# Where in memory the normalised activations of a trunk layer start: 64 and 320 bytes behind a multiple of 512 in place of 0

## The chip, the cores and the metric

The kernel runs on one core of a Trainium2 chip. The metric is the device time in microseconds (us) of one execution; the median of three timed executions of the kernel before is 1382.2 us (1381.91 to 1386.94).

## The reference

One layer of a decoder trunk for 256 positions and 2048 channels, in float32. What matters here is that two normalised activations, `h`, each feed one large projection:

```
mod = (silu(c) @ w_ada + b_ada)                    # six vectors of 2048: shift, scale, gate, twice
h = rms_norm(x, norm1_g) * (1 + scale1) + shift1
proj = h @ w_in + b_in                             # 2048 -> 8192: a_val, a_gate, u, v, g_A, g_B
y_a = silu(layer_norm(dwconv31(a_val * sigmoid(a_gate)))) @ w_conv_out
y_b = (u * spatial_mix(layer_norm(v))) @ w_sgu_out # u, v after GELU
merged = sigmoid(g_A) * y_a + sigmoid(g_B) * y_b
x = x + gate1 * (merged @ w_out)
h = rms_norm(x, norm2_g) * (1 + scale2) + shift2
up = dwconv3(h @ w_up)                             # 2048 -> 11264
x = x + gate2 * ((silu(gt) * val) @ w_down)        # 5632 -> 2048
return rms_norm(x, final_g)
```

## The kernel before

**Split operands.** A float32 product is made from TensorE products of float32r parts: every operand is split into a high part (ScalarE, L145) and a low part (VectorE, L146), and a product is three matmuls: high by high, high by low, low by high (`mm3`, L166 to L170; `mm3a`, L172 to L176). Weights come in tiles of 128 x 2048 (1 MB) by DMAs that SyncE issues (`load_raw`, L148; four buffers), and `load_split` (L155) makes their parts (tags `hi` and `lo`, three buffers each).

**h as the streamed operand.** The activations lie channel by channel: `hH` and `hL` hold 16 tiles of 128 channels x 256 positions, 1024 bytes for each tile in each partition. In the first projection a slice of 128 weight columns (512 bytes in a partition) is loaded into the array, and 256 columns of `hH` or `hL` are streamed past it: "pa" (L168 to L170, convolution branch), "pvc" and "pv" (v), "pu" (u), "pg" (gates). In the up-projection (`mm_up`, L669) the two parts of the second `h` lie side by side for each k (`h2[k]` is 2 x 256 columns): a high weight slice streams all 512 columns (L672), a low one the 256 of the high part (L673). In the output and the down projection (`proj_T`, L563) it is the other way round: slices of the activations (`mH`, `mL`, or the feed-forward's `f`) are loaded into the array, and 512 columns of the weights are streamed.

**Places.** `place(shape, dt, tag, name)` (L80) takes one tile from a pool with one buffer for each tag; tiles of one tag follow each other in the same bytes. `PADS` puts 384 bytes ahead of the first of them, tag T0, which thereby starts at byte 1536 = 3 x 512 of a partition. All the large tiles have sizes in multiples of 512 bytes, so all start at a multiple of 512: `hH` at 42,496 = 83 x 512, `hL` 16,384 bytes behind it, the weight buffers `raw`, `hi` and `lo` from 117,248 = 229 x 512 on. Tag `hH` holds in turn `hH`, `mH` (merged activations), the first half of the second `h`, and `kept0`, a weight tile of the last stage that is used twice; tag `hL` holds `hL`, `mL`, the second half, and `kept1`.

**Order of the work.** (Times are those of the profile's span.) From 20 to 200 us a loop over the 16 channel tiles makes `h` tile by tile from modulation weights (tag `ada`, multiplied on VectorE, L190) and uses each at once; in its second half each step also does two half tiles of gates. Then v, a, u and the other half of the gates (200 to 426 us), the two branch projections (to 535 us), the output projection "wo" (to 634 us), 24 blocks of the up-projection (to 902 us), a first down-projection (to 1035 us), the other 20 blocks (to 1261 us) and the last down-projection. `pump` puts background work (the taps of the convolution, L316, and the modulation columns, L190) between the blocks, each of them with a cost, so that VectorE's queue carries it in program order beside the splits of the weights.

Of the kernel before, what the change touches and what calls it, by code (L numbers as in the profile page):

```python
# [11 lines left out]
F32R = mybir.dt.float32r  # L12
# [5 lines left out]
P = 128  # L18
D = 2048
S = 256  # L20
NT = S // P
KT = D // P
# [18 lines left out]
HI_BUFS = 3  # L41

PADS = dict(T0=384)


C_C = 0
# [19 lines left out]
def trunk(ctx, tc, xin, cvec, rows, wada, wa0, wa1, wv, wu, wg, wso, wco, wsT, wout, wup0, wup, wdn, out):  # L66
# [8 lines left out]
    def psum(name="ps"):  # L75
        return pp.tile([P, 512], F32, tag="ps", name=name)

    pads = dict(PADS)

    def place(shape, dt, tag, name):  # L80

        if pads.get(tag):
            pad = big.tile([P, pads.pop(tag) // 4], F32, tag=f"pad{tag}", name=f"pad{tag}")
            nc.gpsimd.memset(pad, 0.0)
        return big.tile(shape, dt, tag=tag, name=name)

    def slot(i, shape, name, dt=F32):

        return place(shape, dt, f"T{i}", name)
# [4 lines left out]
    def t2(name):  # L94
        return tp.tile([P, 512], F32, tag="t2", name=name, bufs=4)
# [48 lines left out]
    def split(hi, lo, src):  # L144
        nc.scalar.activation(hi, src, AF.Copy)  # L145
        return nc.vector.tensor_tensor(lo, src, hi.bitcast(F32), op=ALU.subtract)  # L146
# [8 lines left out]
    def load_split(src, name, places=None):  # L155

        raw = load_raw(src, name)
        if places is None:
            hi = wp.tile([P, 2048], F32R, tag="hi", name=f"hi_{name}", bufs=HI_BUFS)
            lo = wp.tile([P, 2048], F32R, tag="lo", name=f"lo_{name}", bufs=HI_BUFS)  # L160
        else:
            hi, lo = places[:, 0, :], places[:, 1, :]
        last["split"] = split(hi, lo, raw)
        return [(hi[:, h * 1024:(h + 1) * 1024], lo[:, h * 1024:(h + 1) * 1024]) for h in range(2)]
# [7 lines left out]
    def mm3a(ps, aH, aL, wH, wL, start, stop, **kw):  # L172

        nc.tensor.matmul(ps, aH, wH, start=start, stop=False, **kw)  # L174
        nc.tensor.matmul(ps, aH, wL, start=False, stop=False, **kw)  # L175
        nc.tensor.matmul(ps, aL, wH, start=False, stop=stop, **kw)  # L176
# [3 lines left out]
    nc.scalar.activation(cact, cv[:, C_C:C_C + KT], AF.Sigmoid)  # L180
    nc.vector.tensor_tensor(cact, cact, cv[:, C_C:C_C + KT], op=ALU.mult)
    cbc = place([P, D], F32, "cbc", "cbc")
    for q in range(4):
        bcast_cols(cbc[:, q * 512:(q + 1) * 512], cact[:, 4 * q:4 * q + 4], 4, f"c{q}")
# [39 lines left out]
    def make_h(hH, hL, src, gs, sh, rrow, name):  # L224
# [2 lines left out]
        nc.scalar.activation(hH, h, AF.Identity, bias=sh)  # L227
        return nc.vector.scalar_tensor_tensor(hL, h, sh, hH.bitcast(F32), op0=ALU.add, op1=ALU.subtract)  # L228

    hH = place([P, KT, S], F32R, "hH", "hH")  # L230
    hL = place([P, KT, S], F32R, "hL", "hL")

# [18 lines left out]
    for k in range(KT):  # L253
        c = slice(k, k + 1)
# [25 lines left out]
    def pump(phase, pe, dve):  # L280

        fill, share = SHARES[phase]
        us = fill * pe - dve
        if not (bg["conv"] and bg["ada"]):
            share = 1.0 if bg["conv"] else 0.0
        for key, part in (("conv", us * share), ("ada", us * (1 - share))):
            credit[key] += part
            while bg[key] and credit[key] >= bg[key][0][0]:
                cost, f = bg[key].pop(0)
                credit[key] -= cost  # L290
                f()
            if not bg[key]:
                credit[key] = 0.0
# [243 lines left out]
    for j in range(8):  # L537
        nc.scalar.activation(ycf[:, j, :], ycf[:, j, :], AF.Silu, scale=cv[:, C_LG + j:C_LG + j + 1], bias=cv[:, C_LB + j:C_LB + j + 1])
        if j % 4 == 3:
            hs = slice(j - 3, j + 1)  # L540
            split(aH[:, hs, :], aL[:, hs, :], ycf[:, hs, :])
    mH = place([P, KT, S], F32R, "hH", "mH")
    mL = place([P, KT, S], F32R, "hL", "mL")
    for j2 in range(8):
        parts = load_split(wco[j2], f"co{j2}")
        ps = psum(f"pco{j2}")
# [16 lines left out]
    def proj_T(blk, groups, aHf, aLf, gate, after, rate, pref, apart=False):  # L563

        groups = list(groups)

        def block(ps, g, parts, ts, first, last):
            for kk in range(4):
                k = 4 * g + kk
                hi, lo = parts[kk // 2]  # L570
                cs = slice((kk % 2) * 512, (kk % 2 + 1) * 512)
                for t in ts:
                    tk = slice(t * P, (t + 1) * P)
                    mm3a(ps[t], aHf(k)[:, tk], aLf(k)[:, tk], hi[:, cs], lo[:, cs], first and kk == 0, last and kk == 3)

        def residual(ps, c, t):
            cs = slice(c * 512, (c + 1) * 512)
            tm = t2(f"res{pref}{c}{t}")
            with tc.high_priority(offset=HURRY):
                nc.vector.tensor_tensor(tm, ps[t], gate()[:, cs], op=ALU.mult)  # L580
                nc.vector.tensor_tensor(x2[t][:, cs], x2[t][:, cs], tm, op=ALU.add)
                after(c, t, cs)

        for c in range(4):
            ps = [psum(f"po{pref}{c}{t}") for t in range(NT)]
            if apart and c == 3:

                kept = {}
                for gi, g in enumerate(groups):
                    places = place([P, 2, 2048], F32R, ("hH", "hL")[gi], f"kept{gi}") if gi < 2 else None  # L590
                    kept[g] = load_split(blk(c, g), f"{pref}{c}_{g}", places)
                    block(ps, g, kept[g], [0], gi == 0, gi == len(groups) - 1)
                residual(ps, c, 0)
                order = groups[:-3:-1] + groups[:2] + groups[2:-2]
                for gi, g in enumerate(order):
                    parts = kept[g] if gi < 4 else load_split(blk(c, g), f"{pref}{c}_{g}again")
                    block(ps, g, parts, [1], gi == 0, gi == len(order) - 1)
                residual(ps, c, 1)
                break
            for gi, g in enumerate(groups):  # L600
                parts = load_split(blk(c, g), f"{pref}{c}_{g}")
                at_end = gi == len(groups) - 1
                for ts in ([0], [1]) if at_end else ([0, 1],):
                    block(ps, g, parts, ts, gi == 0, at_end)
                if rate:
                    pump("wo", 5.15, rate)
                if gi == 0:
                    while later:
                        later.pop(0)()
            with ExitStack() as behind:  # L610
                if c == 3 and pref == "wo":
                    up0.append(load_split(wup0[0], "up00"))
                    behind.enter_context(tc.issue_after(last["split"].ins))
                for t in range(NT):
                    residual(ps, c, t)
# [16 lines left out]
    while len(bg["ada"]) > 2 * KT:  # L632
        bg["ada"].pop(0)[1]()
    proj_T(lambda c, g: wout[c, g], range(4), lambda k: mH[:, k, :], lambda k: mL[:, k, :], get_gate1, after_out, 2.9, "wo")
    drain("ada")

# [8 lines left out]
    while later:  # L645
        later.pop(0)()

    h2 = [place([P, 8, 2, S], F32R, tag, f"h2{tag}") for tag in ("hH", "hL")]

    def h2_of(k):  # L650
        return h2[k // 8][:, k % 8, :, :]
# [80 lines left out]
    def down(groups, after, pref, apart=False):  # L732
        proj_T(lambda c, g: wdn[c, g], groups, lambda k: fH[k], lambda k: fL[k], get_gate2, after, 0, pref, apart)
# [89 lines left out]
```

## Time and profile before

| | before |
|---|---|
| median of the timed runs | 1382.2 us (1381.91 to 1386.94, three runs) |
| the profiled execution's own time | 1381.48 us |
| its span, first to last instruction | 1379.7 us |
| TensorE busy / VectorE busy / ScalarE busy | 1334.1 / 1072.6 / 648.8 us |
| mean granted TensorE clock | 0.987 |
| read from and written to HBM | 347.51 MB, 2.10 MB |

The profiled execution's own time is 1.8 us above its span and 0.7 us below the median. A matmul's busy time in the profile is longer than its share of the stream, since matmuls are pipelined: what a matmul costs is the distance from its start to the next one's start. PE is TensorE's matmuls, PEld its weight loads, DVE VectorE, ACT ScalarE, SP SyncE. A window's row gives the busy time of each engine in it with the number of its instructions, then the granted clock (1.00 is full speed), the mean busy share of the DMA engines, and GB/s.

### The profile page before, as it was taken

Reading aid. Unit: us, or ns where it says so; the run is one execution under the profiler, and the core shown is the slowest. Engines: PE = TensorE matmul, PEld = TensorE weight load, DVE = VectorE, ACT = ScalarE, POOL = GpSimd, SP = SyncE. Lnnn points to the kernel's source line nnn. Section 1 sums busy time; section 2 is a strip of 40 time slices with the busy share of each in tenths; the row PEclk is TensorE's granted clock in tenths of the full one; section 3 lists DMA queues with packets and bytes.
Section 4 is the critical chain, followed back from the end, with each engine's and each line's share of the span. In section 5 each row is a group of like instructions: output and inputs, shape, how many; then the busy total and the mean of one; then the engine's idle time right before and its main releaser. Section 6 shows DMA issues by size and latency. Waiting matters only on the chain.

```text
span 1379.7 us, 19691 instructions
## 1 busy us (share of the span) xinstructions
PE 1334.1 (97%) x8170; PEld 1201.4 (87%) x8170; DVE 1072.6 (78%) x1319; ACT 648.8 (47%) x772; POOL 7.0 (1%) x18
## 2 busy tenths in 40 slices
PE   5789999999999999998999999999999999999997
PEld 4689999999999899887888888888888888888885
DVE  6987789999999699788998887754556766776573
ACT  5244464544551244445555555543335555555351
POOL 0000000000000000000000000000000000000000
PEclk9899999999999999999999999999999999999998
DMA  9999977677776799895887774555555555555551
GB/s 351 382 366 326 335 306 272 229 290 270 293 284 246 278 347 345 329 341 216 308 302 279 289 287 183 185 181 197 199 184 187 189 190 190 189 184 183 189 207 61
DMA packets 49481, 350.89 MB, mean 254 GB/s; under 512 B 5488, under 2 KB 5488, under 8 KB 8432
## 3 DMA queue, kind: packets, MB, share of 16 engines
q1 hardware_dynamic: 49392, 349.63, 68.0%
q8 instruction: 64, 1.05, 0.3%
q14 instruction: 25, 0.20, 0.0%
HBM read 347.51 MB, written 2.10 MB: 253 GB/s over the span
## 4 chain that ended last, share of the span: by engine, by line
PE 93%; DVE 4%; DMA 2%; ACT 1%; issue 0%; POOL 0%; ACTq 0%; POOLq 0%; SPq 0%
PE pup L672 24%; PE pup L673 12%; PE pod L176 6%; PE pod L175 6%; PE pod L174 6%; PE pg L170 4%; PE pg L169 4%; PE pg L168 4%; PE pso L529 4%; PE powo L175 2%; PE powo L176 2%; PE powo L174 2%; DVE ada L190 2%; PE pa L168 2%; PE pa L169 2%; PE pa L170 2%
## 5 line engine op out<-in xcount | busy, mean ns | idle before, releaser
L146 DVE TENSOR_TENSOR lo_up<-raw_up,hi_up 128x2048 fp32r<-128x2048 f32 x88 | 201.6, 2290 | 84.1 <-ACT hi_up L145 84.1
L672 PE MATMUL pup<-h2hH,hi_up 128*128 128x512 f32 x704 | 252.2, 397 | 1.4 <-DVE h2hH L228 1.4
L672 PE MATMUL pup<-h2hL,hi_up 128*128 128x512 f32 x704 | 250.0, 394 | 0.0
L190 DVE SCALAR_TENSOR_TENSOR ada<-ada,cbc 128x2048 f32<-128x2048 f32 x96 | 218.7, 2286 | 15.7 <-DMA ada<-in 7.9
L145 ACT ACTIVATE hi_up<-raw_up 128x2048 fp32r<-128x2048 f32 x88 | 168.8, 1918 | 109.4 <-PE pup L672 83.1
L673 PE MATMUL pup<-h2hH,lo_up 128*128 128x256 f32 x704 | 198.3, 282 | 0.0
L673 PE MATMUL pup<-h2hL,lo_up 128*128 128x256 f32 x704 | 197.4, 280 | 0.0
L146 DVE TENSOR_TENSOR lo_d<-raw_d,hi_d 128x2048 fp32r<-128x2048 f32 x42 | 96.3, 2292 | 92.1 <-ACT hi_d L145 92.1
L672 PEld LDWEIGHTS pup<-h2hH,hi_up 128*128 128x128 f32 x704 | 133.0, 189 | 32.9 <-DVE h2hH L228 1.8
L672 PEld LDWEIGHTS pup<-h2hL,hi_up 128*128 128x128 f32 x704 | 131.9, 187 | 30.8
L170 PE MATMUL pg<-hH,lo_g 128*128 128x256 f32 x512 | 145.0, 283 | 0.4 <-DVE lo_g L146 0.4
L169 PE MATMUL pg<-hL,hi_g 128*128 128x256 f32 x512 | 144.9, 283 | 0.0
L168 PE MATMUL pg<-hH,hi_g 128*128 128x256 f32 x512 | 144.9, 283 | 0.0
L673 PEld LDWEIGHTS pup<-h2hH,lo_up 128*128 128x128 f32 x704 | 134.1, 190 | 0.0
L673 PEld LDWEIGHTS pup<-h2hL,lo_up 128*128 128x128 f32 x704 | 133.0, 189 | 0.0
L145 ACT ACTIVATE hi_d<-raw_d 128x2048 fp32r<-128x2048 f32 x42 | 80.5, 1917 | 107.1 <-PE pod L176 106.1
L175 PE MATMUL pod<-lo_d,f 128*128 128x512 f32 x332 | 129.3, 389 | 0.0
L174 PE MATMUL pod<-hi_d,f 128*128 128x512 f32 x332 | 129.2, 389 | 0.0
L176 PE MATMUL pod<-hi_d,f 128*128 128x512 f32 x332 | 129.2, 389 | 0.0
L170 PEld LDWEIGHTS pg<-hH,lo_g 128*128 128x128 f32 x512 | 98.3, 192 | 0.6 <-DVE lo_g L146 0.6
L168 PEld LDWEIGHTS pg<-hH,hi_g 128*128 128x128 f32 x512 | 98.3, 192 | 0.0
L169 PEld LDWEIGHTS pg<-hL,hi_g 128*128 128x128 f32 x512 | 98.3, 192 | 0.0
(202 smaller groups left out, 2585.4 us busy)
## 6 DMA issues: line engine op xcount, KB each, us to landing
ada<-in SPq DMA_DIRECT2D x96, 1024.0 KB, 5.5
raw_up<-in SPq DMA_DIRECT2D x88, 1024.0 KB, 4.8
raw_d<-in SPq DMA_DIRECT2D x44, 1024.0 KB, 4.8
raw_g<-in SPq DMA_DIRECT2D x32, 1024.0 KB, 5.7
raw_wo<-in SPq DMA_DIRECT2D x16, 1024.0 KB, 4.9
raw_a<-in SPq DMA_DIRECT2D x16, 640.0 KB, 5.6
raw_a<-in SPq DMA_DIRECT2D x8, 1024.0 KB, 4.8
raw_u<-in SPq DMA_DIRECT2D x8, 1024.0 KB, 4.9
```

The lines of the kernel that those rows point to most:

```text
L145: nc.scalar.activation(hi, src, AF.Copy)
L146: return nc.vector.tensor_tensor(lo, src, hi.bitcast(F32), op=ALU.subtract)
L168: nc.tensor.matmul(ps, wH, aH, start=start, stop=False, **kw)
L169: nc.tensor.matmul(ps, wH, aL, start=False, stop=False, **kw)
L170: nc.tensor.matmul(ps, wL, aH, start=False, stop=stop, **kw)
L174: nc.tensor.matmul(ps, aH, wH, start=start, stop=False, **kw)
L175: nc.tensor.matmul(ps, aH, wL, start=False, stop=False, **kw)
L176: nc.tensor.matmul(ps, aL, wH, start=False, stop=stop, **kw)
L190: nc.vector.scalar_tensor_tensor(w, w, 1.0, cbc, op0=ALU.mult, op1=ALU.mult, accum_out=dst)
L529: nc.tensor.matmul(ps[:, half * S:(half + 1) * S], raw[:, c0:c0 + P], uv[:, k, :], start=(k == 0), stop=(k == 7))
L672: nc.tensor.matmul(ps, hi, hk.rearrange("p a s -> p (a s)"), start=(k == 0), stop=(k == KT - 1), skip_group_check=True)
L673: nc.tensor.matmul(ps[:, :S], lo, hk[:, 0, :], start=False, stop=(k == KT - 1), skip_group_check=True)
```

## The change

The two tags become one, `hh`, of 8192 + 128 float32 columns (33,280 bytes, 65 x 512), and a helper cuts two areas of 16,384 bytes out of it that start at a chosen byte. The first `h` starts 64 bytes behind a multiple of 512, the second 320 bytes, the merged activations and the kept weights at 0. All four users name it:

```
+H_AT, H2_AT = 64, 320
...
+    def pair(names, by, inner=(S,)):
+
+        t = place([P, 8192 + 128], F32R, "hh", "_".join(names))
+        two = [t[:, by // 4 + i * 4096:by // 4 + (i + 1) * 4096] for i in range(2)]
...
-    hH = place([P, KT, S], F32R, "hH", "hH")
-    hL = place([P, KT, S], F32R, "hL", "hL")
+    hH, hL = pair(("hH", "hL"), H_AT)
...
-    mH = place([P, KT, S], F32R, "hH", "mH")
-    mL = place([P, KT, S], F32R, "hL", "mL")
+    mH, mL = pair(("mH", "mL"), 0)
...
+                room = pair(("kept0", "kept1"), 0, (2048,))
...
-    h2 = [place([P, 8, 2, S], F32R, tag, f"h2{tag}") for tag in ("hH", "hL")]
+    h2 = pair(("h2a", "h2b"), H2_AT, (2, S))
```

The tile itself stays at 42,496. What lies behind it moves by 512 bytes, so every other large tile still starts at a multiple of 512, and the small ones keep their distance from one. Each engine issues the same instructions in the same order, with waits on the same engines and DMA queues: nothing but addresses differs between the two programs.

More of the change, by code (lines that the diff above doesn't have):

```diff
@@ L85, in place @@
         return big.tile(shape, dt, tag=tag, name=name)
+    def pair(names, by, inner=(S,)):
+        t = place([P, 8192 + 128], F32R, "hh", "_".join(names))
+        two = [t[:, by // 4 + i * 4096:by // 4 + (i + 1) * 4096] for i in range(2)]
+        if len(inner) == 1:
+            return [x.rearrange("p (a b) -> p a b", b=inner[0]) for x in two]
+        return [x.rearrange("p (a b c) -> p a b c", b=inner[0], c=inner[1]) for x in two]
     def slot(i, shape, name, dt=F32):
@@ L588, in proj_T @@
                 kept = {}
+                room = pair(("kept0", "kept1"), 0, (2048,))
                 for gi, g in enumerate(groups):
-                    places = place([P, 2, 2048], F32R, ("hH", "hL")[gi], f"kept{gi}") if gi < 2 else None
+                    places = room[gi] if gi < 2 else None
                     kept[g] = load_split(blk(c, g), f"{pref}{c}_{g}", places)
```

## The prediction

> **What bounds the kernel now.** The page comes first: the share of TensorE in the span and in the chain of work that ended last.
>
> ```profile
> PE 1334.1 (97%) x8170; PEld 1201.4 (87%) x8170; DVE 1072.6 (78%) x1319; ACT 648.8 (47%) x772; POOL 7.0 (1%) x18
> PE 93%; DVE 4%; DMA 2%; ACT 1%; issue 0%; POOL 0%; ACTq 0%; POOLq 0%; SPq 0%
> L672 PE MATMUL pup<-h2hH,hi_up 128*128 128x512 f32 x704 | 252.2, 397 | 1.4 <-DVE h2hH L228 1.4
> L170 PE MATMUL pg<-hH,lo_g 128*128 128x256 f32 x512 | 145.0, 283 | 0.4 <-DVE lo_g L146 0.4
> ```
>
> TensorE carries 93% of the chain, and its large groups waited 1.4 and 0.4 us in all. So the pace of the matmul stream is the time, wherever another engine could follow a faster one. Whether it could is read by stage, from the windows.
>
> ```profile
> 20.00:113.00 93.00, 74.18 (x518) 70.50 (x519) 83.98 (x98) 31.11 (x30) 0.00 (x0) 0.90 0.97 364
> 113.00:200.00 87.00, 87.00 (x727) 87.00 (x726) 68.76 (x71) 43.71 (x48) 1.56 (x1) 1.00 0.87 324
> 208.00:236.00 28.00, 28.00 (x237) 28.00 (x236) 28.00 (x40) 11.77 (x14) 0.00 (x0) 1.00 0.72 270
> 290.00:330.00 40.00, 40.00 (x336) 40.00 (x335) 39.99 (x58) 19.49 (x21) 0.00 (x0) 1.00 0.77 274
> 340.00:400.00 60.00, 60.00 (x502) 60.00 (x502) 59.64 (x76) 33.26 (x39) 0.00 (x0) 1.00 0.80 297
> 660.00:860.00 200.00, 200.00 (x1155) 176.36 (x1154) 172.18 (x222) 111.94 (x152) 0.00 (x0) 1.00 0.74 275
> 1045.00:1245.00 200.00, 200.00 (x1134) 173.44 (x1133) 139.65 (x177) 109.60 (x141) 0.00 (x0) 1.00 0.52 187
> ```
>
> The columns after the length are PE, PEld, DVE, ACT and POOL. Up to 113 us TensorE has gaps and the DMA engines are 97% busy. From 113 us on TensorE has none. From 200 to 426 us (third to fifth row) VectorE has none either: 28.00 of 28, 39.99 of 40, 59.64 of 60. In the up-projection (last two rows) VectorE has 14% and 30% to spare, and the DMA engines more.
>
> What one matmul costs is the distance between starts. Two starts in the gate stage, with the six between them left out, and two early in the loop, with six left out, where the clock stood at half:
>
> ```profile
> 344.74 0.28 PE L168 MATMUL pg<-hH,hi_g 128*128 128x256 f32 x1
> ...
> 345.58 0.28 PE L169 MATMUL pg<-hL,hi_g 128*128 128x256 f32 x1
> ```
> ```profile
> 59.64 0.41 PE L168 MATMUL pa<-hH,hi_a 128*128 128x256 f32 x1
> ...
> 61.13 0.41 PE L170 MATMUL pa<-hH,lo_a 128*128 128x256 f32 x1
> ```
> ```profile
> 59.60:61.20 1.60, 1.60 (x10) 1.60 (x9) 1.53 (x5) 0.40 (x1) 0.00 (x0) 0.50 0.88 317
> ```
>
> At half clock 256 columns take 1.49 / 7 = 0.2129 us, so at full clock the stream itself would need some 106.4 ns (an estimate: half of it). The gate stage takes 0.84 / 7 = 120.0 ns: **13.6 ns for each matmul are no streaming**, and they are absent at half clock. The up-projection shows the same for its pairs of 512 and 256 columns:
>
> ```profile
> 660.00:860.00 200.00, 200.00 (x578) 107.89 (x577) 1.00 0.74 275
> 1045.00:1245.00 200.00, 200.00 (x567) 106.35 (x567) 1.00 0.52 187
> ```
>
> These are the windows for L672 alone, one such matmul in each pair. A pair takes 200 / 577 = 346.6 ns in the first 24 blocks and 200 / 567 = 352.7 ns in the other 20, where 768 columns need 319.3 by the same estimate: 27.3 and 33.4 ns are lost. Instructions, operands' starts modulo 512 and clock are the same in the two windows, and the other engines do less in the second. So the loss depends on how the weight load and the stream beside it fall against each other in time. Behind a short interruption at 200.6 us it also changes for a while:
>
> ```profile
> 200.97 0.28 PE L169 MATMUL pvc<-hL,hi_v 128*128 128x256 f32 x1
> ...
> 201.80 0.28 PE L170 MATMUL pvc<-hH,lo_v 128*128 128x256 f32 x1
> ```
>
> Seven distances of 0.83 / 7 = 118.6 ns, before the stage settles at 120 again.
>
> **The change part by part.** Only addresses differ, so nothing is removed, added or queued otherwise; each step is a price per instruction.
>
> Writing `h` at another start costs nothing on VectorE and ScalarE, as far as the nearest rows tell: the convolution's taps read `apad` at starts that step by 4 bytes, and their durations hardly spread.
>
> ```profile
> L316 DVE SCALAR_TENSOR_TENSOR yc<-apad,cv,yc x200: 430/479/486, 192.2 to 444.1; 128x256 f32<-128x256 f32 x100
> L228 DVE SCALAR_TENSOR_TENSOR hL<-h,sh,hH x16: 476/479/481, 20.6 to 181.7; 128x256 fp32r<-128x256 f32 x16
> ```
>
> The taps' median of 479 ns is that of the aligned writes of `hL`. If all 32 writes of `h` lost 10 ns it would be 0.3 us. The shift by 512 of all that lies behind, the merged activations and the kept weights keep their places modulo 512: nothing.
>
> What is left is the streamed read of `h` beside the loading of weights. Now both start at a multiple of 512 each time. A weight slice is 512 bytes; the stream of 256 columns is 1024 bytes. If the two disturb each other where they pass the same place modulo some 512 bytes, they now meet at the start, and the stream, which passes more bytes in the same time, laps the slice once before its end. With a start 64 or 320 bytes on, the first meeting is gone and the lapping is left. That is argued, not seen: no row shows a float32r stream that starts elsewhere. The bounds per matmul: the loss goes (13.6 ns gained), or it grows, by the nearest row as the second up window did against the first (6.1 ns a pair). I take half of it gone, 6.8 ns for each matmul that streams `h`.
>
> The Trainium skill (SBUF — State Buffer, "SBUF: two separate sides" and "Who interferes with whom") says that TensorE reads the streamed operand and the weights through two independent ports, that loading the next weights takes nothing from the running matmul, and that TensorE never waits on anyone. By that rule the start of `h` could not matter, and the sum below would be 0; it is the second rival. The trace speaks against its full form, since the pair's price above moves by 6.1 ns with no change of instruction or start.
>
> The Trainium skill (TensorE: Matmul & The Clock Gate, "Back-to-back issue gap") gives N / 2.4 + 2.5 ns at full clock, 109.2 ns for 256 columns. The gate stage's 120.0 ns do not agree; with that floor instead of 106.4 a full removal would be worth 10.8 and not 13.6 ns.
>
> The sum, stage by stage:
>
> - 20 to 113 us: the DMA engines set the pace, 0.
> - 113 to 200 us: 727 matmuls x 6.8 ns = 4.9 us. The DMA engines must then bring 324 x 87 / 82.1 = 343 GB/s, and the first window shows 364. So 4.9.
> - 200 to 426 us: pvc, pa, pu and pg have 288 + 384 + 384 + 768 = 1824 such matmuls, 12.4 us on TensorE; but VectorE has no gap, and TensorE can only draw nearer to it. How near it is:
>
> ```profile
> L170 PE MATMUL pg<-hH,lo_g x512: 283/283/385, 83.4 to 426.3; 128*128 128x256 f32 x171
> L146 DVE TENSOR_TENSOR lo_g<-raw_g,hi_g x32: 2283/2291/2294, 81.1 to 411.6; 128x2048 fp32r<-128x2048 f32 x32
> L146 DVE TENSOR_TENSOR aL<-yc,aH x2: 1218/1222/1226, 480.9 to 486.4; 128x1024 fp32r<-128x1024 f32 x2
> L168 PE MATMUL pco<-aH,hi_co x128: 278/283/468, 488.7 to 534.5; 128*128 128x256 f32 x128
> ```
>
> The last low part is ready at 411.6 + 2.3 = 413.9 us; its 48 matmuls x 120 ns start at about 426.4 - 5.8 = 420.6. The cushion is 6.7 us, and no more can be gained. At the branch projection the operand `aL` is done at 487.6, 1.1 us ahead of its first use, so some is given back there. I count 4.
> - 634 to 902 us: 24 blocks x 2 x 16 = 768 pairs x 13.65 ns = 10.5 us. VectorE's 172 us in 200 fit into 192.
> - 1035 to 1261 us: 640 pairs from 352.7 to the same 333.0 ns, 19.7 each, 12.6 us.
> - wo, the two down-projections and the branch projections stream other operands: 0.
>
> Together 32.0 us off the profiled execution's 1381.5 leaves 1349.5. It lies 0.7 below the median of the runs shown, so **1350 us**. Behind the up-projection the down stages have TensorE alone on the chain, so what is gained there stays.
>
> **The rivals.**
>
> *All of the loss goes.* For: at half clock there is none. Against: then the lapping would cost nothing either. 727 x 13.6 = 9.9, which the DMA engines' 364 GB/s hold to 9; 5 for 200 to 426 us; 768 x 27.3 = 21.0; 640 x 33.4 = 21.4: 56 us, 1326.
>
> *It doesn't do what it says: the 13.6 ns are a price of each matmul that no start moves.* For: 512-column pairs and 256-column matmuls lose the same per matmul, 27.3 / 2 and 13.6. Against: the second up window and the 118.6 ns. 1382.
>
> *Slower: the stream locks into a worse rhythm.* The second up window shows one, at the same starts. If a start 320 bytes on leads the first 24 blocks into it, 768 x 6.1 = 4.7 us; if the other 20 lose as much again, 640 x 6.1 = 3.9; and 3 ns on each of the 727 + 1824 matmuls that stream the first `h`, which nothing hides since TensorE has no gap there, 7.7. Together 16 us, 1398. It decides from about 5 ns a pair on: 1408 x 5 = 7 us.
>
> **How the numbers follow.** A measurement of this kernel can tell about 0.5% (6.9 us) from no change. Half of the loss gone: 0.50. All gone: 0.13. No effect: 0.20. Slower: 0.17. So faster 0.63, same 0.20, slower 0.17. The forecast's own range is 1335 to 1370 (about three quarters of the loss gone to a quarter). The range of 8 in 10 reaches from 1327, about the case of all gone, up to 1388, over no effect and its 0.5%; it leaves out most of the slower case and a part of the fastest.
>
> **What would show it right or wrong.** Right: in the gate stage the distance between starts falls from 120 to some 113 ns, or at least comes to stand on VectorE's splits, with waits of "pg" for `lo_g`; in both up windows L672 counts about 600 in 200 us; wo and down keep theirs. The half is wrong if the count is 577 and 567 again (no effect), above 620 (all gone) or below 560 (slower). The cap of 200 to 426 us is wrong if that stretch shortens by more than 7 us.

## The result, and the profile after

The changed kernel takes 1376.58 us (median of six, 1374.36 to 1379.05) where the kernel before takes 1384.57 (median of six, 1381.47 to 1389.23): ratio 0.9941, 95% interval 0.9916 to 0.9965. It is faster, as forecast, but by 8 us, a quarter of the 32 that the sum gave: 6.6 us above the upper end of the forecast's own range (1335 to 1370), inside the range of 8 in 10 (1327 to 1388). The profiled execution took 1376.01 us, its span 1374.3.

Start of the page of the changed kernel (its lines stand 9 further on, so L168 to L170 are now L177 to L179, L672 is L680), and the windows that answer to those of before:

```profile
PE 1327.7 (97%) x8170; PEld 1195.6 (87%) x8170; DVE 1073.5 (78%) x1319; ACT 649.8 (47%) x772; POOL 6.9 (1%) x18
PE 93%; DVE 3%; DMA 3%; ACT 1%; issue 0%; POOL 0%; ACTq 0%; POOLq 0%; SPq 0%
```
```profile
20.00:113.00 93.00, 73.05 (x510) 69.55 (x511) 83.72 (x97) 30.49 (x30) 0.00 (x0) 0.89 0.96 359
113.00:200.00 87.00, 87.00 (x741) 87.00 (x740) 70.10 (x71) 44.46 (x49) 1.56 (x1) 1.00 0.88 330
340.00:400.00 60.00, 60.00 (x512) 60.00 (x511) 60.00 (x74) 32.61 (x41) 0.00 (x0) 1.00 0.79 297
```

From 113 us on the same stretches hold more matmuls: 741 for 727, 512 for 502. A window also counts the matmuls that began ahead of it and are still running, 0.28 / 0.12 or some 2.4 of them, so the gate stage goes from 60 / 499.6 = 120.1 ns a matmul to 60 / 509.6 = 117.7. The forecast had 113.2. The up-projection, L680 alone:

```profile
660.00:860.00 200.00, 200.00 (x574) 107.89 (x574) 1.00 0.73 269
1045.00:1245.00 200.00, 200.00 (x575) 107.89 (x574) 1.00 0.53 187
```

578 and 567 counted pairs have become 574 and 575. From start to start a pair takes 348.9 ns in both parts; before it took 346.7 in the first and 353.3 in the second (the prediction's 352.7 took 567 pairs for that window, one too many). So the first part has become slower and the second quicker. The distances between the starts of L680 (L672 before) repeat themselves: 347, 347, 346 ns in the first part of before, 361, 349, 350 in its second, 351, 349, 347 after. Such a repeating pattern is called a rhythm below. From the first starts of the groups in both traces:

| stretch | before, us | after, us | difference |
|---|---|---|---|
| up to the first "pvc" | 200.8 | 200.1 | -0.7 |
| v, a, u, gates | 225.7 | 221.1 | -4.6 |
| so, co, wo | 207.4 | 207.7 | +0.3 |
| up-projection, 24 blocks | 268.5 | 270.9 | +2.4 |
| first down-projection | 132.4 | 132.3 | -0.1 |
| up-projection, 20 blocks | 226.1 | 223.3 | -2.8 |
| rest | 118.8 | 118.9 | +0.1 |
| span | 1379.7 | 1374.3 | -5.4 |

Of the +2.4 us in the first part, 768 x 2.2 ns = 1.7 are the pairs' price. The other 0.7 lie in the first block, whose first pairs run at half clock (640 ns each): it took 445 ns a pair after and 422 before. The first row of the table is uncertain by more than its 0.7 us: over the profiles of all experiments it is 200.8 to 202.4 us with the first `h` at 0 and 198.1 to 200.1 with it at 64.

VectorE did not become the limit. Its cushion in the gate stage:

```profile
L179 PE MATMUL pg<-hH_hL,lo_g x512: 279/280/384, 84.9 to 421.1; 128*128 128x256 f32 x171
L155 DVE TENSOR_TENSOR lo_g<-raw_g,hi_g x32: 2287/2302/2924, 82.6 to 410.1; 128x2048 fp32r<-128x2048 f32 x32
```

The last low part is ready at 412.4, its 48 matmuls begin at 421.1 - 48 x 0.1177 = 415.5: 3.1 us of the 6.7 are left, and "pg" waited 0.4 us in all for `lo_g`, as before.

### The profile page after: what moved, and what is told of

Same layout as the page of the kernel before. It is cut to its first block, busy times and chain, and to the rows that moved or that the text cites. A ratio compares the mean times of both kernels' runs of the same rounds, so it can differ in the third digit from the quotient of the medians.

```text
span 1374.3 us, 19691 instructions
## 1 busy us (share of the span) xinstructions
PE 1327.7 (97%) x8170; PEld 1195.6 (87%) x8170; DVE 1073.5 (78%) x1319; ACT 649.8 (47%) x772; POOL 6.9 (1%) x18
## 4 chain that ended last, share of the span: by engine, by line
PE 93%; DVE 3%; DMA 3%; ACT 1%; issue 0%; POOL 0%; ACTq 0%; POOLq 0%; SPq 0%
PE pup L680 24%; PE pup L681 12%; PE pod L184 6%; PE pod L183 6%; PE pod L185 6%; PE pg L179 4%; PE pg L177 4%; PE pg L178 4%; PE pso L537 4%; PE powo L184 2%; PE powo L185 2%; PE powo L183 2%; DVE ada L199 2%; PE pa L179 2%; PE pa L177 2%; PE pa L178 2%
## 5 line engine op out<-in xcount | busy, mean ns | idle before, releaser
L680 PE MATMUL pup<-h2a_h2b,hi_up 128*128 128x512 f32 x1408 | 494.1, 395 | 0.9 <-DVE h2a_h2b L237 0.9
L681 PE MATMUL pup<-h2a_h2b,lo_up 128*128 128x256 f32 x1408 | 395.7, 281 | 0.0
L680 PEld LDWEIGHTS pup<-h2a_h2b,hi_up 128*128 128x128 f32 x1408 | 266.3, 189 | 62.7 <-DVE h2a_h2b L237 1.3
L681 PEld LDWEIGHTS pup<-h2a_h2b,lo_up 128*128 128x128 f32 x1408 | 265.0, 188 | 0.0
L179 PE MATMUL pg<-hH_hL,lo_g 128*128 128x256 f32 x512 | 143.2, 280 | 0.4 <-DVE lo_g L155 0.4
L177 PE MATMUL pg<-hH_hL,hi_g 128*128 128x256 f32 x512 | 143.1, 279 | 0.0
L178 PE MATMUL pg<-hH_hL,hi_g 128*128 128x256 f32 x512 | 142.8, 279 | 0.0
L179 PEld LDWEIGHTS pg<-hH_hL,lo_g 128*128 128x128 f32 x512 | 96.2, 188 | 0.6 <-DVE lo_g L155 0.6
L178 PEld LDWEIGHTS pg<-hH_hL,hi_g 128*128 128x128 f32 x512 | 96.0, 187 | 0.0
L177 PEld LDWEIGHTS pg<-hH_hL,hi_g 128*128 128x128 f32 x512 | 95.9, 187 | 0.0
L177 PE MATMUL pa<-hH_hL,hi_a 128*128 128x256 f32 x256 | 72.1, 300 | 19.6 <-ACT hH_hL L236 19.6
L155 DVE TENSOR_TENSOR lo_g<-raw_g,hi_g 128x2048 fp32r<-128x2048 f32 x32 | 74.5, 2328 | 18.5 <-ACT hi_g L154 18.5
L324 DVE SCALAR_TENSOR_TENSOR yc<-apad,cv,yc 128x256 f32<-128x256 f32 x200 | 85.7, 495 | 0.2
```

Of the source, the lines that this page charges most:

```text
L177: nc.tensor.matmul(ps, wH, aH, start=start, stop=False, **kw)
L178: nc.tensor.matmul(ps, wH, aL, start=False, stop=False, **kw)
L179: nc.tensor.matmul(ps, wL, aH, start=False, stop=stop, **kw)
L324: nc.vector.scalar_tensor_tensor(ycf[:, j, :], src, cv[:, w0 + k:w0 + k + 1], ycf[:, j, :], op0=ALU.mult, op1=ALU.add)
L680: nc.tensor.matmul(ps, hi, hk.rearrange("p a s -> p (a s)"), start=(k == 0), stop=(k == KT - 1), skip_group_check=True)
L681: nc.tensor.matmul(ps[:, :S], lo, hk[:, 0, :], start=False, stop=(k == KT - 1), skip_group_check=True)
```

## The experiments

Theory A: a float32r stream and the loading of the next weights disturb each other by their distance in memory and by their distance in time; the start changes a small part of the loss, and the up-projection's pairs have several rhythms. The rivals are named in the expectations. Eight kernels are timed against before, in three batches of five rounds, each beside executions of before of its own; four are streams without the layer, profiled once. So every price of a pair or a matmul is that of one profiled execution.

### One step alone

The edits are the one line, in turn (both at 0; only the first moved; only the second moved):

```
-H_AT, H2_AT = 64, 320
+H_AT, H2_AT = 0, 0       # zero
+H_AT, H2_AT = 64, 0      # h64
+H_AT, H2_AT = 0, 320     # h2only
```

> One place, but both h at 0: only the merging of the two tags and the shift of all that lies behind by 512 bytes are left. Theory A (the start of the streamed operand against the weights' changes a small part of what each matmul loses): as before, 120.0 ns a matmul in the gate stage, pairs of the up-projection at 346.6 or 352.7 ns, a time within 0.3% of before. Rival B (the one place or the shift by 512 did it): 117.7 ns and 348.5 ns as in the changed kernel, some 8 us faster.

Measured: ratio 0.9993 (0.9976 to 1.0010), the gate stage at 120 ns and pairs at 346.7 and 353.3. Rival B falls: the one place and the shift by 512 do nothing that can be measured.

> Only the first h moved, to 64; the second at 0. Theory A: 117.7 ns in the gate stage, and pairs in one of the rhythms of before, 346.6 or 352.7 ns; some 5 us faster than before where the rhythms are the same. Rival B: the same as with both at 0.

Measured: ratio 0.9952 (0.9931 to 0.9973), median 1375.92. The gate stage of zero and then of h64:

```profile
340.00:400.00 60.00, 60.00 (x502) 60.00 (x502) 59.81 (x77) 31.70 (x38) 0.00 (x0) 1.00 0.80 297
```
```profile
340.00:400.00 60.00, 60.00 (x512) 60.00 (x511) 59.82 (x74) 32.77 (x39) 0.00 (x0) 1.00 0.77 285
```

502 matmuls as before, and 512 as in the changed kernel: 117.7 ns. The stretch of v, a, u and gates took 225.7 and 221.1 us.

> Only the second h moved, to 320; the first at 0. Theory A: 120.0 ns in the gate stage, 348.5 ns for every pair in both parts of the up-projection: 1.5 us lost in the first 24 blocks and 2.7 gained in the other 20 against the profile of before, so about 1 us faster, and up to 6 us faster than an execution of before in which both parts run at 352.7. Rival B: as with both at 0.

Measured: ratio 0.9988 (0.9972 to 1.0004), median 1384.01. The first part was not at 348.5 but at 353.3 ns, the second at 348.9. The windows of L680 (L672's heir), of h64 and then of h2only:

```profile
660.00:860.00 200.00, 200.00 (x578) 107.87 (x578) 1.00 0.73 269
1055.00:1245.00 190.00, 190.00 (x539) 101.05 (x538) 1.00 0.53 189
```
```profile
660.00:860.00 200.00, 200.00 (x567) 106.36 (x566) 1.00 0.74 273
1055.00:1245.00 190.00, 190.00 (x545) 102.42 (x545) 1.00 0.53 189
```

567 pairs in the first part of h2only, where the changed kernel, with the same second start, has 574. As far as the times can tell, the whole of the gain comes from the first `h`; the second start of 320 has no effect that can be told from none, and two prices of its own.

### Streams without the layer

Matmuls alone, all operands ready beforehand; a case is a pair of starts, and each is interrupted by 128-column transposes. The core of the first of them:

```
for name, form, h, w in PLAN:
    for part in range(2):
        upset(name)                       # a 128-column transpose
        for b in range(8):
            ...
            for k in range(4):            # hi, lo: weights at WA[w]; hk: h at HA[h]
                ...
                nc.tensor.matmul(ps[:, :S], hi, hk[:, 0, :], ...)
                nc.tensor.matmul(ps[:, :S], hi, hk[:, 1, :], ...)
                nc.tensor.matmul(ps[:, :S], lo, hk[:, 0, :], ...)
```

> A stream of its own that computes nothing of the layer: 256-column float32r matmuls in threes as in the gate stage, with no other engine at work, 192 for each case, interrupted twice by one 128-column transpose; h at 0, 32, 64, 128, 192, 256, 320, 384, 448 with the weights at 0; then weights at 64 with h at 0, 64, 128, and weights at 448 with h at 0. Theory A (the two reads disturb each other by their distance modulo 512): 120.0 ns at 0, 117.7 at 64; h and weights both at 64 give 120.0, h at 128 with weights at 64 117.7. Rival C (the start counts by itself): h and weights both at 64 give 117.7, h at 0 with weights at 64 120.0. Rival D (what is lost comes from the other engines' and the DMAs' traffic): 109 ns or less in all cases.

The starts of the two transposes of a case, 96 matmuls apart, in the trace: h at 64 with weights at 0, then both at 64, then h at 0 with weights at 64.

```profile
56.91 0.27 PE L120 MATMUL zca<-ident,xs 128*128 128x128 f32 x1
...
68.33 0.27 PE L120 MATMUL zca<-ident,xs 128*128 128x128 f32 x1
```
```profile
239.97 0.27 PE L120 MATMUL zcc<-ident,xs 128*128 128x128 f32 x1
...
251.59 0.27 PE L120 MATMUL zcc<-ident,xs 128*128 128x128 f32 x1
```
```profile
217.54 0.27 PE L120 MATMUL zac<-ident,xs 128*128 128x128 f32 x1
...
228.55 0.27 PE L120 MATMUL zac<-ident,xs 128*128 128x128 f32 x1
```

11.42, 11.62 and 11.01 us: with both at 64 the stream is as slow as with both at 0 (308.89 to 320.51, 11.62 too), 0.20 / 96 = 2.1 ns a matmul slower than with h alone at 64. So the distance counts, not the start (rival C falls), and other engines' traffic is not needed (rival D falls). Mean distances between starts behind the first 24 of a part:

| h minus weights, bytes | 256 columns, ns |
|---|---|
| 0, 256 | 120.0 |
| 64, 192, 320, 448 | 117.8 |
| 128, 384 | 118.6 |
| 32 | 116.7 |
| -64 (weights moved) | 113.3 in one part, 117.8 in the other |

> As the first stream with 256 columns in threes, finer: h at 0, 16, 32, 48, 64, 80, 96, 224, 480 with weights at 0, then h at 0 with weights at 32, 64 and 128; three interruptions for each. Theory A: 120 ns at 0, between 116 and 119.5 elsewhere, h at 224 like h at 480 (they differ by 256), weights moved up by 64 like h moved to 192 or 448. If the loss could all go at some start, one of these cases would be near 107 to 109 ns; theory A with a fixed part expects none under 113.

Measured: 16 and 32: 116.7; 48, 224, 480 and weights at 32: 118.3 to 118.4; 80 and 96: 120.0; weights at 128: 118.7; h at 64, and weights at 64: 117.8 or 113.3, by the interruption. Nothing is under 113.3. The starts 48 (116 to 119.5 expected, 118.4 found) and 224 (like 480) came out by theory A; 80 and 96, with the full 120.0, and the 113.3 did not.

> A stream that computes nothing of the layer, no other engine at work: pairs of a 512- and a 256-column float32r matmul as in the up-projection, 72 pairs for each case after each of three interruptions (one, two, three 128-column transposes), h at 0, 32, 64, 128, 192, 256, 320, 384, 448 and weights at 0; then 512-column matmuls alone, as in the down-projection, h at 0, 64, 128, 256, 320; then pairs at 0 once more. Theory A (distance modulo 256 between stream and weights sets the loss, and the pairs have several rhythms that an interruption can switch): pairs of 346.6 or 353 ns at 0 and at 256, 349 or 353 ns at 320 and at 64, and 192 and 448 like 64; 512 columns alone 226.7 ns at 0 and 256 and some 2 ns less at 64 and 320. Rival E (each start has one price, and the two prices in the kernel come from what the other engines do): one value for each case, whatever the interruption.

Measured, over whole pairs: 346.7 or 353.3 ns at 0 and at 256, by the interruption; 346.7 at 32 after all three; 353.3 at 64, 192, 320 and 448; 351.1 at 128 and 384. 512 columns alone: 226.7 at 0 and 256, 228.9 at 64 and 320, some 232 at 128, so dearer, not cheaper as expected. Pairs at 0 behind two and behind three transposes, 15 and 16 pairs apart, and at 32, 16 pairs:

```profile
425.31 0.40 PE L137 MATMUL spz<-ha,wa 128*128 128x512 f32 x1
...
430.61 0.40 PE L137 MATMUL spz<-ha,wa 128*128 128x512 f32 x1
```
```profile
433.75 0.39 PE L137 MATMUL spz<-ha,wa 128*128 128x512 f32 x1
...
439.30 0.39 PE L137 MATMUL spz<-ha,wa 128*128 128x512 f32 x1
```
```profile
41.20 0.39 PE L137 MATMUL spb<-hb,wa 128*128 128x512 f32 x1
...
46.75 0.39 PE L137 MATMUL spb<-hb,wa 128*128 128x512 f32 x1
```

5.30 / 15 = 353.3, 5.55 / 16 = 346.9, 5.55 / 16 = 346.9. Same program lines, same addresses, no other engine at work, two prices: rival E falls. The number of transposes does not choose between them: behind three, 0 gave 353.3 in the first case and 346.7 in the last. At 320, the second start of the change, the pair is at the dearer price after all three.

> Where the part of the loss comes from that no start moves. Streams of float32r matmuls of 256 columns with weight slices of 128, 96, 64 and 32 columns (the array is filled in part, the product is a smaller one), then slices of 128 with 128, 192, 384 and 512 streamed columns, then h at 64 with slices of 128 and of 32; last bfloat16 operands, 256 columns, slices of 128 and 32. Theory F (the loss is paid for each weight slice that is read beside the stream, by its bytes): 120 ns at 128, some 116 at 96, 113 at 64, 110 at 32; the same 13.6 ns at 384 and 512 columns as at 256. Rival G (a price of each float32r matmul, whatever its weights): 120 ns at all four, 13.6 ns everywhere. bfloat16: half the bytes, 113 ns by F; no statement by G.

Measured: slices of 128, 96, 64, 32 columns: 120.0, 116.1, 113.3, and 120.0 or 117.8 ns. 128 and 192 streamed columns both 111.7, 384: 173.3, 512: 226.7 ns (in the last two some 14 above what 106.4 ns for each 256 columns would make). h at 64: 117.8 with slices of 128, 113.3 to 116.7 with 32. bfloat16: 109.2 with either slice. Theory F holds from 128 down to 64 columns, falls at 32, where it expected 110, and misses bfloat16, where it expected 113; G falls at 96 and 64. Neither said that 128 and 192 streamed columns would cost the same. In bfloat16, two starts with 64 matmuls from the one to the transpose that ends the part:

```profile
273.07 0.27 PE L140 MATMUL sbx<-hb,wb 128*128 128x256 bf16 x1
...
280.06 0.27 PE L117 MATMUL zbx<-ident,xs 128*128 128x128 f32 x1
```

6.99 / 64 = 109.2 ns. The formula of the Trainium skill (TensorE: Matmul & The Clock Gate, "Back-to-back issue gap"), which that page calls the gap of an isolated matmul, gives the same 109.2 ns for 256 columns; in these streams bfloat16 agrees with it, float32r at 113.3 to 120.0 does not.

### Rhythms and starts in the kernel

```
-H_AT, H2_AT = 64, 320
+H_AT, H2_AT = 32, 0      # h32
+H_AT, H2_AT = 32, 32     # both32
+H_AT, H2_AT = 0, 32      # h2at32
```
```
+    nudge = psum("nudge")                # with 64, 0; n is 1 (nudge1) or 3 (nudge3)
+    for _ in range(n):
+        nc.tensor.transpose(nudge[:, :P], cv[:, :P], ident)
     for p in range(SEG, NF):
         up(p)
```

> The first h at 64, the second at 0, and one 128-column transpose of a constant ahead of the 25th block of the up-projection, where the kernel took 353.3 ns a pair in every profile so far; no address differs from the kernel with 64 and 0. Theory A (the rhythm that a pair falls into is set by how the stream begins): the other 20 blocks may take 346.6 instead, 4.3 us less, or another value; a change of the pair's price at equal addresses. Rival E (the price of the second part comes from the other engines' work beside it): 353.3 as before, 0.1 us more for the transpose.

Measured: median 1375.44 (1371.41 to 1382.8), ratio 0.9931 (0.9904 to 0.9958). In its profile the second part takes 346.7 ns:

```profile
660.00:860.00 200.00, 200.00 (x578) 107.87 (x578) 1.00 0.73 270
1055.00:1245.00 190.00, 190.00 (x550) 102.50 (x549) 1.00 0.53 189
```

550 in 190 us where h64 had 539. In the four profiles with the second `h` at 0 and no transpose there (before, zero, h64, h32) the second part begins alike, with distances of 340, 350, 361, 349, 350 ns, and stays at 353.3. Behind the transpose it begins with 436, 352, 347, 346 and stays at 346.7. So the one transpose switched the rhythm of 20 blocks in this execution.

> As the one before with three transposes; in the stream without other work three of them led into 346.4 ns in one case of two. Theory A: 346.6 or 353.3, 4.3 us less in the first case. Rival E: 353.3, 0.3 us more.

Measured: median 1374.5, ratio 0.9930 (0.9907 to 0.9953); in its profile both parts are at 353.3. By the times neither nudge can be told from h64: a nudge can switch, but does not choose. Of nudge3's six times the profiled one, with its first part in the slow rhythm, is 1381.48; the other five lie from 1372.88 to 1375.59.

> The first h at 32 in place of 64, the second at 0. In the stream without other work 32 gave 116.7 ns after every interruption, 64 117.8. Theory A: 116.7 ns in the gate stage, so 3.3 ns on 2551 matmuls that nothing but VectorE's cushion of 6.7 us caps: some 7 us faster than before where the up-projection takes the same rhythms, 1 to 2 us faster than 64. Rival H (the stream's order of three in the kernel differs enough, so no such carry-over): 117.8 or 120 ns.

Measured: ratio 0.9924 (0.9898 to 0.9949), median 1374.68. The gate stage had 516 matmuls in 60 us, 116.8 ns, as in the stream, so rival H falls; v, a, u and gates took 219.8 us, 1.3 less than in h64. Both parts of the up-projection had 353.3 in the profile. The times alone don't tell h32 from h64.

> Both at 32. The pairs gave 351.5 ns after all three interruptions in the stream without other work. Theory A: 351.5 in both parts of the up-projection, in every execution, so the times spread less than with the second at 0, and the median is 2 to 4 us above the best executions of that one. Rival H: two values again.

(The 351.5 in it was misread, a mean over an odd number of distances; the rows of the pairs at 32 give 346.9, so this forecast started from a wrong price and missed.) Measured: median 1369.39 (1367.69 to 1371.03), **ratio 0.9885 (0.9865 to 0.9905)**, the quickest of all; the gate stage and the pairs:

```profile
340.00:400.00 60.00, 60.00 (x512) 60.00 (x511) 60.00 (x74) 32.67 (x39) 0.00 (x0) 1.00 0.78 285
```
```profile
660.00:860.00 200.00, 200.00 (x578) 108.33 (x577) 1.00 0.73 269
1055.00:1245.00 190.00, 190.00 (x549) 102.85 (x549) 1.00 0.54 191
```

346.7 ns in both parts. The gates took 117.7 ns here and 116.8 in h32, at the same start: they have more than one price too.

> Only the second h moved, to 32, the first at 0: what the up-projection gives by itself. Theory A (at 32 the kernel's pairs have one rhythm, the quick one): 120.0 ns in the gate stage, 346.7 ns in both parts in every execution; 4.3 us less than the best executions of before, some 1377 us, and little spread. Rival I (346.7 in both parts was one draw of several): 346.7, 353.3 or 351.5 in the profile, and times in two groups some 4 or 5 us apart.

Measured: ratio 0.9953 (0.9935 to 0.9972), six times from 1377.29 to 1380.12. Its profile has 578 and 549 again. Rival I falls as far as five rounds can tell: with the second `h` at 32 the times no longer lie in two groups.

How the times spread fits the rhythms. Of the 28 executions of before beside the first experiments, 15 lie from 1379.9 to 1384.0 and 13 from 1385.7 to 1389.7; the price of the first part in its two rhythms differs by 768 x 6.6 ns = 5.1 us. That the upper group has the slow rhythm in its first part is argued from this and from nudge3's profile; only profiled executions show the rhythm itself.

## Why the forecast was right in its sign and wrong in its size

- **The stream of TensorE is the time, and the start of `h` matters.** Right for the first `h`: zero against h64 shows it, and the rival of no effect falls. The Trainium skill (SBUF — State Buffer, "Who interferes with whom") gives TensorE an independent read port for the weights. Read as saying that the places of the two operands don't matter, it does not agree with this case: 120.0 ns with both at 64, 117.8 with `h` alone at 64.
- **"I take half of it gone, 6.8 ns for each matmul that streams `h`": this step failed.** At 64 the loss fell by 2.2 to 2.4 ns, a third of that (117.7 ns in the gate stage, where some 113 was named as the sign of being right). Of the 13.6 ns, 2.8 are there in bfloat16 too (109.2 against 106.4), and at no start that was tried did a float32r matmul of 256 columns with full slices take under 113.3. The picture behind the half, two meetings of which one goes, gave no number; it stood in the place of a measurement, and the streams do not bear it out: at 256 the loss is that of 0, and at 80 and 96 it is whole again.
- **The up-projection, 10.5 + 12.6 us: this step failed most.** These are 23.1 of the sum's 32 us, and the profile showed 0.4. The step took both windows' losses as a stock that the start would halve. They are two rhythms of the same start, and at 320 no price under 348.9 ns was seen: 353.3 in the stream alone, 353.3 and 348.9 in the kernel. A 512-column matmul by itself even loses there, 228.9 ns against 226.7 at 0. That the two parts came to +2.4 and -2.8 us and nearly cancelled is chance: with the same second start h2only had 353.3 in its first part. The rival "locks into a worse rhythm" described this mechanism; the changed kernel met it in its first part, by 2.2 ns a pair.
- **113 to 200 us, 4.9 us, and 200 to 426 us, 4 us.** With 2.3 ns the first is 727 x 2.3 = 1.7. The profile shows 0.7 at its end, since the changed kernel was behind at 113 us (510 matmuls for 518 from 20 us on). The second would be 1824 x 2.3 = 4.2 and measured 4.6: the sum's 4 came out right by luck, since it rested on a cap, VectorE's cushion, that was never reached.
- **No effect on wo, down and the writes of `h`.** Right, as the table of stretches shows.
- **The base.** The profile of before had caught the quick rhythm in its first part, so its 1381.5 us was in the lower of two groups. The median of before is 3 us higher, which is most of the difference between 5.4 us by profile and 8.0 by medians.

What exactly delays a matmul is not shown: that the loading of the next weights is the partner of the stream is argued from the distance between `h` and weights and from the width of the slice. Why 349 ns shows at 320 in the kernel and not in the stream, why 80 and 96 bytes cost as much as 0, why slices of 32 columns are dearer than of 64, and what in the memory makes the distance count modulo 256, stay open.

## What to carry to other kernels

Where a matmul stream is the bound, measure the distance between starts against the same stream in bfloat16 or at another start before halving a loss on paper. For the 256-column matmuls a stream alone, profiled once in an execution of 0.3 ms, gave the 117.8 ns that the sum had guessed at 113; for the pairs at 320 it gave 353.3, which in the two kernels with that start only one part in four shows; the others are at 348.9. Two prices for the same instructions are a sign of rhythms; then one profile of each kernel is one draw. Look for a start that keeps its cheap price after every interruption: for the pairs that was 32 bytes here (346.7 ns), and it gave the quickest kernel.

## What the hardware showed unexpectedly

- Float32r matmuls of 256 columns take 113.3 to 120.0 ns by the distance of stream and weights, alike at distances that differ by 256 bytes; of 512 columns 226.7 at 0 and 256, 228.9 at 64 and 320, and some 232 at 128. Of the starts tried with both, those that help the narrow stream (64, 128, 320) hurt the wide one.
- A stream keeps its rhythm for hundreds of microseconds (346.7 or 353.3 ns a pair over 20 blocks), and one 128-column transpose, worth 0.1 us, can switch it.
- With slices of 128 columns, 128 streamed columns cost as much as 192: 111.7 ns.
